# Two-layer trunk kernel: eight pairs of 512-column blocks with a quarter of the contraction by Strassen's scheme

## The chip, the cores and the metric

One Trainium2 chip, one of its cores. The metric is the device time of one execution in microseconds (us); lower is better. The kernel before took 873.62 us in the median of three runs (873.49 to 875.35). Engines: TensorE (PE, its weight loads PEld), VectorE (DVE), ScalarE (ACT), GpSimd (POOL) and SyncE (SP). PE sums its products in PSUM, which has 8 banks of 128 x 512 fp32 numbers.

## The reference

Two layers of a trunk on 256 tokens of width 2048, all in fp32. Layer 0 mixes tokens by differential attention, layer 1 by chunked gated linear attention (GLA). Each layer is `x <- x + W_out(mixer(RMSNorm(x)) * silu(gate))`; cut to the products that matter here:

```python
q, k, v, g = split(h @ w_in, 4)              # layer 0: 2048 x 8192
y = o * silu(g); x = x + y @ w_out           # 2048 x 2048
q, k, v, g, lr = split(h @ w_in, ...)        # layer 1: 1024, 1024, 2048, 2048, 16
o_t = q_t @ state_t                          # state_t = decay * state + k^T v, chunks of 64
x = x + (rmsnorm(o) * silu(g)) @ w_out       # 2048 x 2048
```

## The kernel before, in words

Tokens lie in two halves of 128 (t = 0, 1). A contraction of 2048 is 16 tiles of 128. Every fp32 operand of a product is split into a high part and a remainder, both fp32r: activations once (`aT`, then `bT` in the same memory, and `y`, the input of an out projection, which layer 1 calls `z`), weights as they stream in. `weights()` (L93 to 102) loads a chunk of 128 x 2 x 512 fp32 (two contraction tiles of a block of 512 columns, 512 KB) by a DMA from SP into `raw`, copies it to `hi` on ACT (L100) and writes `lo = raw - hi` on DVE (L101). `raw`, `hi` and `lo` have four buffers each. `stream` (L128 to 132) lists the chunks in the order of use: the four column groups of layer 0's q, k and v, four blocks of its gate, four of its out projection, then k and q, values, gate and out projection of layer 1.

`project()` (L158 to 196) makes one block: two banks of a pool of four (`pj`), one for each half of the tokens, and for each contraction tile and half three matmuls of 128 x 512: high activations by `hi` (L178), remainders by `hi` (L179), high activations by `lo` (L180). That is 96 matmuls a block. k and q of layer 1 are made transposed (L182, L184). While a block runs, `pump()` issues steps of a background list of generators (attention, transposes of x, decay gates, GLA).

After a block its two banks are evacuated: in `gate()` (L431 to 451) by a tanh on ACT (L436) and two products on DVE (L437, L439), then four transposes on PE (L442) and a split of the result (L445 to 451); in an out projection of layer 0 by an addition of x on DVE (L528), after which `transpose_x` (L506 to 522) puts the new x into `bT`; in values by a scaled copy on ACT and a remainder on DVE (L725, L726), after which `gla_values` (L675 to 690) multiplies the attention weights `ATh`, `ATl` with the values into `ps_o` (L681). The last out projection adds x and stores. The last block finishes its bank of t = 0 ahead of the other (`tail`).

The stages follow each other as written, but the order on each engine is set by a scheduler, which goes by priorities (the place in the program) and a timeline of its own; each engine then runs its queue in order. The next block takes the two other banks of the pool:

```python
banks = [bank(pj, "pj"), bank(pj, "pj")]     # L161, pool pj has 4
...
hi, lo = next_weights()                      # L168, one chunk is split ahead
```

Of the kernel before, what the change touches and what calls it, by code (L numbers as in the profile page):

```python
# [16 lines left out]
P = 128  # L17
S = 256
# [11 lines left out]
WARM = 10  # L30


@with_exitstack
def trunk_kernel(
# [29 lines left out]
    pj = ctx.enter_context(tc.tile_pool(name="pj", bufs=4, space=bass.MemoryType.PSUM))  # L64
# [3 lines left out]
    def bank(pool, name):  # L68
        return pool.tile([P, 512], F32, tag=pool.name, name=name)

# [56 lines left out]

    stream = [lambda c=c: first_weights(c) for c in range(NCK)]  # L128
    for w in (aw, awo, bwkq, bwvg, bwo):
        for i in range(w.shape[0]):  # L130
            ck = CK * NB // w.shape[3]
            stream += [w[i, :, k:k + ck, :] for k in range(0, KT, ck)]
# [25 lines left out]
    def project(lhs, token_major, steps=0, before=None, tail=False):  # L158


        banks = [bank(pj, "pj"), bank(pj, "pj")]  # L161
# [3 lines left out]
        for c in range(n):  # L165
# [3 lines left out]
            for kk in range(ck):  # L169
                k = c * ck + kk  # L170
                first, last = k == 0, k == KT - 1
                for t in range(2):
                    sl = slice(t * P, (t + 1) * P)
                    if tail and c == n - 1:
                        continue
# [10 lines left out]
            if tail and c == n - 1:  # L186
                for t in range(2):
                    for kk in range(ck):
                        xh, xl = (lhs[c * ck + kk][:, i, t * P:(t + 1) * P] for i in range(2))
                        nc.tensor.matmul(banks[t], lhsT=xh, rhs=hi[:, kk, :], start=False, stop=False)  # L190
                        nc.tensor.matmul(banks[t], lhsT=xl, rhs=hi[:, kk, :], start=False, stop=False)
                        nc.tensor.matmul(banks[t], lhsT=xh, rhs=lo[:, kk, :], start=False, stop=kk == ck - 1)
# [3 lines left out]
        return banks  # L196

# [10 lines left out]
    def square_sum(blk, pool):  # L208
        for t in range(2):
            jk = pool.tile([P, NB], F32, tag="sq", name="sq", bufs=2 if pool is ta else 1)  # L210
            nc.scalar.activation(jk, xk[:, t, blk * NB:(blk + 1) * NB], AF.Square, accum_out=ssq[:, t, blk:blk + 1])
# [29 lines left out]
    for i in range(2):  # L241
        kl = ta.tile([P, 2, 4, S], F32R, name=f"kl{i}", bufs=1)
# [188 lines left out]
    def gate(banks, o, rh, dst, blk, gains):  # L431

        for t in range(2):
# [10 lines left out]
            yh, yl = (dst[blk // 2][:, blk % 2 * 4:blk % 2 * 4 + 4, i, t * P:(t + 1) * P] for i in range(2))  # L444
            if gains is not None:  # L445
                nc.scalar.activation(yh, ptv, AF.Copy, scale=gains)
                nc.vector.scalar_tensor_tensor(out=yl, in0=ptv, scalar=gains, in1=yh.bitcast(F32),
                                               op0=ALU.mult, op1=ALU.subtract)
            else:
                nc.scalar.activation(yh, ptv, AF.Copy)  # L450
                nc.vector.tensor_tensor(out=yl, in0=ptv, in1=yh.bitcast(F32), op=ALU.subtract)
# [39 lines left out]
    y = None  # L491
    for hg in range(4):
        b = project(aT, True, steps=8)
        if y is None:
            y, yT = operand(["y0", "y1"])
        if hg == 1:
            drain()
        gate(b, o_a[hg], r1h, y, hg, gsub)
    lay_a.close()


    tb_stack = ExitStack()
    tb_ = tb_stack.enter_context(tc.tile_pool(name="tb_", bufs=2))
    _, bT = operand(["aT"])

    def transpose_x(blk):  # L506
        square_sum(blk, tb_)
        yield
        for half in range(2):
            pt = bank(ptr, "pt_x")  # L510
            for j in range(2):
                k = blk * 4 + half * 2 + j
                for t in range(2):
                    nc.tensor.transpose(pt[:, (j * 2 + t) * P:(j * 2 + t + 1) * P], xk[:, t, k * P:(k + 1) * P], ident)
            for j in range(2):
# [8 lines left out]
    for blk in range(4):  # L524
        b = project(yT, True, steps=4)
        cols = slice(blk * NB, (blk + 1) * NB)
        for t in range(2):
            nc.vector.tensor_tensor(out=xk[:, t, cols], in0=b[t], in1=xk[:, t, cols], op=ALU.add)  # L528
        background.append(transpose_x(blk))
# [172 lines left out]


# [9 lines left out]
    for h in range(BH):  # L713
        b = project(bT, False, steps=3)
# [4 lines left out]
    for h in range(BH):  # L719
        b = project(bT, True, steps=4)  # L720
        drain()
        vh = tb_.tile([P, 2, NB], F32R, tag="t4", name="vh", bufs=5)
        vl = tb_.tile([P, 2, NB], F32R, tag="t4", name="vl", bufs=5)
        for t in range(2):
            nc.scalar.activation(vh[:, t, :], b[t], AF.Copy, scale=r2[:, t:t + 1])  # L725
            nc.vector.scalar_tensor_tensor(out=vl[:, t, :], in0=b[t], scalar=r2[:, t:t + 1],  # L726
                                           in1=vh[:, t, :].bitcast(F32), op0=ALU.mult, op1=ALU.subtract)
        v = (vh, vl)
        o = big.tile([P, 2, NB], F32, tag="o", name="ob", bufs=4)
        o_b[h] = o  # L730
        background.append(gla_values(h, v, o))
# [77 lines left out]
```

## Time and profile before

| what | before |
|---|---|
| median of 3 runs | 873.62 us (873.49 to 875.35) |
| the profiled execution | 872.59 us |
| its span in the profile | 870.5 us |
| PE busy | 865.2 us, 99%, 4156 matmuls and transposes |
| DVE busy | 546.1 us, 63%, 824 instructions |
| ACT busy | 468.3 us, 54%, 745 instructions |
| POOL busy | 108.2 us, 12% |
| DMA | 164.40 MB, mean 189 GB/s |

The span runs from the first to the last instruction that the profile shows; the profiled execution's own time holds 2.1 us more. A share is busy time over the span. Matmuls are pipelined, and the duration of one counts its tail: the rows of a busy PE overlap, and the pitch of matmuls is read from their starts. All times in the trace count from the start of the span. A row of the timeline gives start, duration, engine, line, operation and operands (partitions x elements); in brackets behind it stands how long the engine had been idle before, and whose work ended that.

### The profile page before, as it was taken

To read this page: it belongs to the slowest core of one execution; us is meant where nothing else is said; L and a number is where in the kernel's file an instruction comes from. 1 tells how busy PE (TensorE), PEld (TensorE's weight loads), DVE (VectorE), ACT (ScalarE), POOL (GpSimd) and SP (SyncE) were. 2 spreads that over 40 slices of the span, in tenths; PEclk is the share of its full clock that TensorE was granted. 3 is DMA by queue.
4 is the path that set the end of the run, shared out by engine and by line. 5 is a ranking of instruction groups with operands and counts; after the bars stand their busy time and mean duration, and the time that the engine had idled before them with its cause. 6 is when DMAs were issued, how large, how long until landed. Compare 5 with 4: busy or idle time off the path is not lost.

```text
span 870.5 us, 11443 instructions
## 1 busy us (share of the span) xinstructions
PE 865.2 (99%) x4156; PEld 721.8 (83%) x4156; DVE 546.1 (63%) x824; ACT 468.3 (54%) x745; POOL 108.2 (12%) x142
## 2 busy tenths in 40 slices
PE   9999999999999999999999999999999999999998
PEld 6788888888888888888888888888888888888886
DVE  7766775687677676666655658945555565665552
ACT  7756566566656765554545549533444444444331
POOL 3330221023123000103000012300000000000000
PEclk9999999999999999999999999999999999999999
DMA  8886666566665555666666544655565656666771
GB/s 344 292 283 203 182 187 196 180 178 196 186 177 171 182 152 158 197 182 203 200 190 179 182 144 156 200 163 177 172 177 170 183 177 178 189 182 202 211 224 50
DMA packets 47206, 164.40 MB, mean 189 GB/s; under 512 B 5904, under 2 KB 6432, under 8 KB 47152
## 3 DMA queue, kind: packets, MB, share of 16 engines
q1 hardware_dynamic: 43568, 155.47, 58.5%
q0 software_dynamic: 2288, 6.38, 2.5%
q10 hardware_dynamic: 1296, 1.85, 0.6%
q8 instruction: 32, 0.52, 0.2%
q14 instruction: 22, 0.18, 0.1%
HBM read 161.55 MB, written 5.27 MB: 192 GB/s over the span
## 4 chain that ended last, share of the span: by engine, by line
PE 98%; DMA 1%; ACT 0%; DVE 0%; SPq 0%; DVEq 0%; issue 0%
PE pj L178 27%; PE pj L180 27%; PE pj L179 26%; PE pj L182 7%; PE pj L184 3%; PE ps_o L681 1%; PE ps_at L667 1%; PE ps_s L366 1%; PE pt_qk L333 1%; PE pt_y L442 1%; PE ps_s L364 1%; DMA xw<-in_xw 1%; PE pt_a L395 1%; PE po L404 0%; PE ps_lr L578 0%; PE po L406 0%
## 5 line engine op out<-in xcount | busy, mean ns | idle before, releaser
L101 DVE TENSOR_TENSOR lo<-raw,hi 128x1024 fp32r<-128x1024 f32 x280 | 344.0, 1230 | 220.3 <-ACT hi L100 219.7
L100 ACT ACTIVATE hi<-raw 128x1024 fp32r<-128x1024 f32 x280 | 296.2, 1059 | 294.7 <-PE pj L179 246.7
L178 PE MATMUL pj<-hi,aT 128*128 128x512 f32 x768 | 302.8, 396 | 0.0
L180 PE MATMUL pj<-lo,aT 128*128 128x512 f32 x768 | 299.6, 392 | 0.1
L179 PE MATMUL pj<-hi,aT 128*128 128x512 f32 x768 | 299.5, 391 | 0.0
L180 PEld LDWEIGHTS pj<-lo,aT 128*128 128x128 f32 x768 | 144.2, 188 | 30.2 <-DVE lo L124 0.5
L178 PEld LDWEIGHTS pj<-hi,aT 128*128 128x128 f32 x768 | 144.7, 188 | 29.3 <-ACT hi L100 0.6
L179 PEld LDWEIGHTS pj<-hi,aT 128*128 128x128 f32 x768 | 144.7, 188 | 28.7
L178 PE MATMUL pj<-hi,y 128*128 128x512 f32 x252 | 98.9, 392 | 0.0
L180 PE MATMUL pj<-lo,y 128*128 128x512 f32 x252 | 98.3, 390 | 0.0
L179 PE MATMUL pj<-hi,y 128*128 128x512 f32 x252 | 98.1, 389 | 0.0
L182 PE MATMUL pj<-aT,hi 128*128 128x512 f32 x256 | 90.7, 398 | 0.0
L184 PE MATMUL pj<-aT,lo 128*128 128x256 f32 x256 | 71.8, 281 | 0.0
L182 PEld LDWEIGHTS pj<-aT,hi 128*128 128x128 f32 x256 | 48.0, 188 | 11.3
L180 PEld LDWEIGHTS pj<-lo,y 128*128 128x128 f32 x252 | 47.3, 188 | 9.9
L179 PEld LDWEIGHTS pj<-hi,y 128*128 128x128 f32 x252 | 47.3, 188 | 9.6
L178 PEld LDWEIGHTS pj<-hi,y 128*128 128x128 f32 x252 | 47.3, 188 | 9.5
L184 PEld LDWEIGHTS pj<-aT,lo 128*128 128x128 f32 x256 | 48.3, 189 | 0.3
L221 POOL TENSOR_TENSOR rq<-ms,mhalf 128x8 f32<-128x8 f32 x16 | 38.3, 2398 | 34.8 <-DVE ms L323 34.8
L701 POOL TENSOR_TENSOR kq<-kq,rb 128x256 f32<-128x256 f32 x16 | 18.1, 1140 | 75.5 <-DVE kq L699 75.5
L221 POOL TENSOR_TENSOR f<-zz,mhalf 128x2 f32<-128x2 f32 x16 | 11.3, 706 | 91.4 <-DVE zz L413 91.3
L355 POOL DMA_DIRECT2D tb<-skew_d x16 | 9.3, 582 | 96.6 <-DVE nm L371 44.4
(178 smaller groups left out, 681.2 us busy)
## 6 DMA issues: line engine op xcount, KB each, us to landing
raw<-in_aw SPq DMA_DIRECT2D x120, 512.0 KB, 3.7
raw<-in_bwvg SPq DMA_DIRECT2D x64, 512.0 KB, 3.6
raw<-in_awo SPq DMA_DIRECT2D x32, 512.0 KB, 3.6
raw<-in_bwkq SPq DMA_DIRECT2D x32, 512.0 KB, 4.1
raw<-in_bwo SPq DMA_DIRECT2D x32, 512.0 KB, 3.7
xw<-in_xw SPq DMA_DIRECT2D x10, 384.0 KB, 11.4
skew_d<-bias_d POOLq DMA_DIRECT2D x8, 384.0 KB, 6.5
xw<-in_xw SPq DMA_DIRECT2D x3, 768.0 KB, 7.9
```

What stands on the lines that cost most here:

```text
L100: nc.scalar.activation(hi, raw, AF.Copy)
L101: nc.vector.tensor_tensor(out=lo, in0=raw, in1=hi.bitcast(F32), op=ALU.subtract)
L178: nc.tensor.matmul(banks[t], lhsT=xh, rhs=hi[:, kk, :], start=first, stop=False)
L179: nc.tensor.matmul(banks[t], lhsT=xl, rhs=hi[:, kk, :], start=False, stop=False)
L180: nc.tensor.matmul(banks[t], lhsT=xh, rhs=lo[:, kk, :], start=False, stop=last)
L182: nc.tensor.matmul(banks[t], lhsT=hi[:, kk, sl], rhs=lhs[k].rearrange("p a s -> p (a s)"), start=first, stop=False, skip_group_check=True)
L184: nc.tensor.matmul(banks[t][:, 0:S], lhsT=lo[:, kk, sl], rhs=lhs[k][:, 0, :], start=False, stop=last, skip_group_check=True)
L221: nc.gpsimd.tensor_tensor(out=dst, in0=src, in1=mhalf[:, 0:n], op=ALU.pow)
L333: nc.tensor.transpose(pt[:, h * P:(h + 1) * P], qn[:, h * P:(h + 1) * P], ident)
L355: nc.gpsimd.dma_start(tb, bass.AP(tensor=skew_d.tensor, offset=skew_d.offset + (hg * 4 + h) * 384 + 127, ap=[[AH * 384 - 1, P], [1, S]]))
L364: nc.tensor.matmul(pss[t][:, c0:c0 + n], lhsT=q, rhs=qk[:, 8 + t * 4 + h, 0:n], start=True, stop=False)
L701: nc.gpsimd.tensor_tensor(out=dst, in0=dst, in1=rb, op=ALU.mult)
```

## The change

Blocks of the two out projections, of values and of the gate of layer 1 are made as pairs of two adjacent blocks L and L + 1, eight pairs in all. In each pair four of the 16 contraction tiles form a 2 x 2 scheme: token halves by pairs of tiles (A11, A12, A21, A22), and the pairs of tiles by blocks (B11, B12, B21, B22). Strassen's scheme in Winograd's form needs 7 products there instead of 8; a product is 128 x 256 by 256 x 512, six matmuls. The other 12 tiles are made as before (`plain`). Sums on the weight side (u2, u3, and sums in the place of b12 and b22, L246 to 253) are made on DVE from fp32 chunks, and 7 chunks are split where 4 were. Sums on the activation side are made once per mixer (`sums`, in `gate` for the out projections, in `quarter_sums` for values and gate). Four banks with names p0 to p3 take the place of the pool:

- `c` and `e` are the two banks of a group g, `b` and `d` the banks of the other group. `p1` makes the first product in `c` and copies its negative to `b` on ACT (L288). `p7` makes another in `e` and copies it to `s7` in SBUF on ACT (L294).
- `run` adds a product to `c`, makes `d = s7 - c` on DVE (L300), adds to `b`, then alternates plain tiles of the left block (`b`, `d`) with products in `c`; it makes `e = c - s7` on DVE (L307). The left block is evacuated, then the 12 plain tiles of the right block go to `c` and `e`. In the middle of them `p1` and `p7` of the next pair are issued. Group g alternates, so `b` of the next pair is the bank that is `c` of this one.
- The four copies between banks stand under a scheduler priority that is AHEAD = 80 places earlier.
- The memory of layer 0's pool `ta` is held until its out projection has ended, so that loads of layer 1's small weights (`lr_raw` and others, L547 ff. before) come later. Contraction tiles of `awo`, `bwvg` and `bwo` are reordered on the host, and the program's `dynamic_dma_scratch_size` is set to 4096.

The core of the diff (line numbers as L288 count in the changed kernel):

```diff
+AHEAD = 80
-    pj = ctx.enter_context(tc.tile_pool(name="pj", bufs=4, space=bass.MemoryType.PSUM))
+    pj = ctx.enter_context(tc.tile_pool(name="pj", bufs=1, space=bass.MemoryType.PSUM))
...
+    def pj_bank(g, i):
+        return pj.tile([P, 512], F32, tag=f"p{2 * g + i}", name="pj")
...
+    class Pair:
+        def __init__(self, w, L, lhs, S, N, neg, comb, special, left, right):
...
+            n0, n1 = [[self.chunk(i, 2 + c) for c in range(6)] for i in range(2)]
+            self.head = [self.job1, lambda: split(self.u3)]
+            self.mid = [lambda: split(self.u2), self.job2, n0[0], lambda: split(self.b12), n0[1],
+                        lambda: split(self.b22), n0[2], lambda: split(self.u2), *n0[3:]]
+            self.rest = n1
...
+        def load(self):
+            self.b12, self.b22, self.u3, self.u2 = self.special()
+            nc.sync.dma_start(self.b12, self.chunk(1, 0))
+            nc.sync.dma_start(self.b22, self.chunk(1, 1))
...
+        def job1(self):
+            raw, r = self.raw(0)
+            nc.vector.tensor_tensor(out=self.u3, in0=self.b12, in1=self.b22, op=ALU.add)
+            nc.vector.tensor_tensor(out=self.u2, in0=self.u3, in1=raw, op=ALU.add)
+            nc.vector.tensor_tensor(out=self.b12, in0=self.b12, in1=raw, op=ALU.add)
+            return r
...
+        def p1(self):
+            g = self.g = group[0]
+            group[0] = 1 - g
+            self.c, self.e = pj_bank(g, 0), pj_bank(g, 1)
+            self.part(self.c, self.neg, start=True)
+            self.b = pj_bank(1 - g, 0)
+            with tc.high_priority(offset=AHEAD):
+                nc.scalar.activation(self.b, self.c, AF.Copy, scale=-1.0)
+
+        def p7(self):
+            self.part(self.e, lambda j: self.comb(2, j), start=True)
+            self.s7 = gp.tile([P, NB], F32, tag="s7", name="s7", bufs=1)
+            with tc.high_priority(offset=AHEAD):
+                nc.scalar.activation(self.s7, self.e, AF.Copy)
+
+        def run(self, after=None, steps=(1, 1, 1, 1, 1, 1), tail=False):
+            self.part(self.c, lambda j: self.comb(1, j))
+            self.d = pj_bank(1 - self.g, 1)
+            with tc.high_priority(offset=AHEAD):
+                nc.vector.scalar_tensor_tensor(out=self.d, in0=self.c, scalar=-1.0, in1=self.s7,
+                                               op0=ALU.mult, op1=ALU.add)
+            self.part(self.b, self.quarter(1, 0), stop=False)
+            left, right = (self.b, self.d), (self.c, self.e)
+            self.plain(left, 0, True, steps[0])
+            self.part(self.c, lambda j: self.comb(0, j))
+            with tc.high_priority(offset=AHEAD):
+                nc.vector.tensor_tensor(out=self.e, in0=self.c, in1=self.s7, op=ALU.subtract)
+            self.plain(left, 1, False, steps[1])
+            self.part(self.c, lambda j: self.comb(3, j), stop=False)
+            self.plain(left, 2, False, steps[2])
+            self.part(self.d, self.quarter(1, 1), stop=False)
+            for i in range(3, 6):
+                if i == 4 and after is not None:
+                    after.load()
+                self.plain(left, i, False, steps[i])
+            self.left(left)
+            for i in range(6):
+                if after is not None and i == 4:
+                    after.p1()
+                elif after is not None and i == 5:
+                    after.p7()
+                self.plain(right, i, tail and i == 5, steps[i])
+            self.right(right)
...
+    for p, q in zip(pairs_b, pairs_b[1:] + [None]):
+        p.run(q, steps=(1, 1, 1, 1, 0, 0), tail=q is None)
...
+    nc = _bacc.Bacc("TRN2", target_bir_lowering=False, num_devices=1, dynamic_dma_scratch_size=4096)
```

**The order on PE between two projects of values.** A row is a line, an instruction, its output and inputs with shape, and what it waits for; `pj` are banks, a number behind a name tells buffers apart. Before, from the last rows of one block (pj_5632 is its second bank) to the next:

```order
L178 MATMUL pj_5632<-hi_5769,aT_3825 128x512
L179 MATMUL pj_5632<-hi_5769,aT_3825 128x512
L180 MATMUL pj_5632<-lo_5770,aT_3825 128x512
L178 MATMUL pj_5811<-hi_5787,aT_3825 128x512 [waits Activation_49]
L179 MATMUL pj_5811<-hi_5787,aT_3825 128x512
L180 MATMUL pj_5811<-lo_5788,aT_3825 128x512 [waits DVE_49]
L178 MATMUL pj_5812<-hi_5787,aT_3825 128x512
```

Now, from the last rows of the first pair (pj_5485 is `e`) to the second pair (pj_5865 is its `c`; `cb` holds the activations' sums; `ps_o`, `vh`, `vl` belong to the GLA step of the block before):

```order
L276 MATMUL pj_5485<-hi_5898,aT_3877 128x512
L277 MATMUL pj_5485<-hi_5898,aT_3877 128x512
L278 MATMUL pj_5485<-lo_5899,aT_3877 128x512
L895 MATMUL ps_o_5977<-vh_5927,ATh_4593 128x512 [waits Activation_49]
L895 MATMUL ps_o_6018<-vh_5927,ATh_4593 128x512
L895 MATMUL ps_o_5977<-vl_5928,ATh_4593 128x512 [waits DVE_49]
L895 MATMUL ps_o_5977<-vh_5927,ATl_4594 128x512
L895 MATMUL ps_o_6018<-vl_5928,ATh_4593 128x512
L895 MATMUL ps_o_6018<-vh_5927,ATl_4594 128x512
L895 MATMUL ps_o_6018<-vh_5927,ATh_4593 128x512 [waits Activation_49]
L263 MATMUL pj_5865<-hi_5911,cb_2939 128x512 [waits Activation_49]
L265 MATMUL pj_5865<-hi_5911,cb_2939 128x512
```

The next block's first row waited for its split; now the row that adds to `c` waits for ACT, whose copy reads `c`, and seven rows of the GLA step stand between.

**The order on ACT and DVE between two gates of layer 1** (the third block, where the second pair of gates begins). `th` is the tanh and then the gated output, `r2h` the token scale, `ob` the GLA output, pj_6536 and pj_6537 the banks of the block that ends. Before, ACT:

```order
L436 ACTIVATE th_6682<-pj_6536,r2h_4641 128x512 [waits PE_49]
L100 ACTIVATE hi_6743<-raw_6742 128x1024 [waits DMAHW5_49,DVE_49,PE_49]
L436 ACTIVATE th_6693<-pj_6537,r2h_4641 128x512 [waits PE_49]
L100 ACTIVATE hi_6761<-raw_6760 128x1024 [waits DMAHW6_49,DVE_49,PE_49]
L100 ACTIVATE hi_6779<-raw_6778 128x1024 [waits DMAHW7_49,DVE_49,PE_49]
```

and DVE:

```order
L101 TENSOR_TENSOR lo_6726<-raw_6724,hi_6725 128x1024 [waits DMAHW4_49,PE_49,Activation_49]
L437 SCALAR_TENSOR_TENSOR th_6682<-th_6682,ob_5990 128x512 [waits Activation_49]
L439 SCALAR_TENSOR_TENSOR th_6682<-pj_6536,r2h_4641,th_6682 128x512 [waits DVE_49]
L101 TENSOR_TENSOR lo_6744<-raw_6742,hi_6743 128x1024 [waits DMAHW5_49,PE_49,Activation_49]
L437 SCALAR_TENSOR_TENSOR th_6693<-th_6693,ob_5990 128x512 [waits Activation_49]
```

Now (pj_6238 and pj_6239 are `c` and `e` of the first pair, pj_6620 and pj_6621 those of the second; pj_6634, the second pair's `b`, is the bank of pj_6238; `comb` and `cf` are sums of the gated output, `special` holds weight sums), ACT:

```order
L294 ACTIVATE s7_6664<-pj_6621 128x512 [waits PE_49]
L592 ACTIVATE th_6682<-pj_6238,r2h_4719 128x512 [waits PE_49]
L142 ACTIVATE hi_6731<-special_5434 128x1024 [waits DVE_49,PE_49]
L592 ACTIVATE th_6693<-pj_6239,r2h_4719 128x512 [waits PE_49]
L582 ACTIVATE comb_6503<-cf_6538 128x4x128 [waits DVE_49]
L288 ACTIVATE pj_6634<-pj_6620 128x512 [waits DVE_49]
```

and DVE:

```order
L335 TENSOR_TENSOR cf_6538<-pt_y_6509,cf_6538 128x128 [waits DVE_49]
L593 SCALAR_TENSOR_TENSOR th_6682<-th_6682,ob_5933 128x512 [waits Activation_49]
L246 TENSOR_TENSOR special_6836<-special_6834,special_6835 128x1024
L143 TENSOR_TENSOR lo_6732<-special_5434,hi_6731 128x1024 [waits PE_49,Activation_49]
L595 SCALAR_TENSOR_TENSOR th_6682<-pj_6238,r2h_4719,th_6682 128x512 [waits DVE_49]
```

On ACT the copy of `c` to `b` (L288) now stands behind both tanh of the block that ends and a split; on DVE a weight sum and a split stand between the two products that read pj_6238.

## Rows read from the trace of the kernel before

**Rows 1.** The page, parts 1 and 2: busy time, and the clock in 40 slices.
```profile
PE 865.2 (99%) x4156; PEld 721.8 (83%) x4156; DVE 546.1 (63%) x824; ACT 468.3 (54%) x745; POOL 108.2 (12%) x142
...
PE   9999999999999999999999999999999999999998
...
PEclk9999999999999999999999999999999999999999
```

**Rows 2.** The page, part 4: the chain that ended last, by engine.
```profile
PE 98%; DMA 1%; ACT 0%; DVE 0%; SPq 0%; DVEq 0%; issue 0%
```

**Rows 3.** Busy time by window, first output projections, then values to end.
```profile
core 0: us, PE busy (x) PEld busy (x) DVE busy (x) ACT busy (x) POOL busy (x), PEclk, DMA share, GB/s
408.00:500.00 92.00, 92.00 (x435) 76.64 (x434) 54.27 (x65) 47.20 (x67) 5.67 (x12) 1.00 0.63 189
600.00:866.00 266.00, 266.00 (x1204) 220.85 (x1203) 142.64 (x147) 113.96 (x131) 4.34 (x8) 1.00 0.60 176
```

**Rows 4.** Timeline of PE in an output projection: start, duration, engine, line.
```profile
446.63 0.39 PE L179 MATMUL pj<-hi,y 128*128 128x512 f32 x1
...
449.35 0.39 PE L179 MATMUL pj<-hi,y 128*128 128x512 f32 x1
```

**Rows 5.** Who waited for whom: us in total, times, longest.
```profile
ACT hi L100 <- PE pj L179: 246.7, 163, 2.1
```

**Rows 6.** Groups of instructions on ACT: busy us, mean ns, idle before.
```profile
L100 ACT ACTIVATE hi<-raw 128x1024 fp32r<-128x1024 f32 x280 | 296.2, 1059 | 294.7 <-PE pj L179 246.7 <-PE pj L182 17.1 <-issue 12.5
...
L698 ACT ACTIVATE kq<-pj 128x256 f32<-128x256 f32 x16 | 6.0, 376 | 12.0 <-PE pj L184 12.0
...
L725 ACT ACTIVATE vh<-pj,r 128x512 fp32r<-128x512 f32 x8 | 5.5, 686 | 4.9 <-PE pj L180 4.9
...
L450 ACT ACTIVATE y<-pt_y 128x512 fp32r<-128x512 f32 x8 | 4.7, 590 | 1.2 <-PE pt_y L442 1.2
```

**Rows 7.** Groups of instructions on DVE, same columns.
```profile
L101 DVE TENSOR_TENSOR lo<-raw,hi 128x1024 fp32r<-128x1024 f32 x280 | 344.0, 1230 | 220.3 <-ACT hi L100 219.7 <-PE pj L179 0.3
...
L439 DVE SCALAR_TENSOR_TENSOR th<-pj,r2h,th 128x512 f32<-128x512 f32 x8 | 6.0, 752 | 0.3
...
L528 DVE TENSOR_TENSOR xk<-pj,xk 128x512 f32<-128x512 f32 x8 | 5.4, 688 | 0.0
```

**Rows 8.** The page, part 6: DMA issues, KB each, us to landing.
```profile
raw<-in_bwvg SPq DMA_DIRECT2D x64, 512.0 KB, 3.6
```

**Rows 9.** Timeline behind a project's last matmul: a gate, of PE, ACT and DVE.
```profile
754.67 0.39 PE L180 MATMUL pj<-lo,aT 128*128 128x512 f32 x1
...
755.10 0.69 ACT L436 ACTIVATE th<-pj,r2h 128x512 f32<-128x512 f32 x1 [1.21 <-PE pj L180]
755.68 1.05 ACT L100 ACTIVATE hi<-raw 128x1024 fp32r<-128x1024 f32 x1
756.63 0.68 ACT L436 ACTIVATE th<-pj,r2h 128x512 f32<-128x512 f32 x1
...
755.82 0.69 DVE L437 SCALAR_TENSOR_TENSOR th<-th,ob 128x512 f32<-128x512 f32 x1 [0.67 <-ACT th L436]
756.54 0.75 DVE L439 SCALAR_TENSOR_TENSOR th<-pj,r2h,th 128x512 f32<-128x512 f32 x1
```

**Rows 10.** Timeline of PE around four transposes, and around three state products.
```profile
786.72 0.60 PE L442 MATMUL pt_y<-ident,th 128*128 128x128 f32 x4
...
787.39 0.39 PE L178 MATMUL pj<-hi,y 128*128 128x512 f32 x1
...
620.36 0.39 PE L681 MATMUL ps_o<-vh,ATh 128*128 128x512 f32 x1
...
621.04 0.39 PE L178 MATMUL pj<-hi,aT 128*128 128x512 f32 x1
```

**Rows 11.** Timeline of PE at the start: the warm-up matmuls.
```profile
1.23 4.45 PE L81 MATMUL ps_idle<-zero 128*128 128x512 bf16 x10 [1.23 <-DVE zero L78]
```

More of the change, by code (lines that the diff above doesn't have):

```diff
@@ L156, in drain, with project @@
             pump()
-    def project(lhs, token_major, steps=0, before=None, tail=False):
-        banks = [bank(pj, "pj"), bank(pj, "pj")]
+    def project(lhs, token_major, steps=0, before=None):
+        banks = [pj_bank(group[0], i) for i in range(2)]
+        group[0] = 1 - group[0]
         n = NCK if token_major else NCK // 2
@@ L185, in project @@
                                          start=False, stop=last, skip_group_check=True)
[L186 to L192, printed above, removed]
             want = (c + 1) * steps // n
@@ L490, in trunk_kernel @@
         background.append(attention(hg, qk, kl, v, o))
[L491 to L504, printed above, removed]
     def transpose_x(blk):
-        square_sum(blk, tb_)
+        square_sum(blk, gp)
         yield
@@ L521, in transpose_x @@
                                                in1=bT[k][:, 0, :].bitcast(F32), op0=ALU.mult, op1=ALU.subtract)
-            yield
[L524 to L529, printed above, removed]
+                if blk == 0:
+                    nc.scalar.activation(af[:, 2 * j:2 * j + 2, :].rearrange("p a s -> p (a s)"), p, AF.Copy, scale=g)
@@ new lines, in trunk_kernel, with add_x, f, neg_in_place @@
+    cb = big.tile([P, 2, 5, 2, P], F32R, tag="cb", name="cb")
+    def add_x(blk):
+        def f(banks):
+            cols = slice(blk * NB, (blk + 1) * NB)
+            for t in range(2):
+                nc.vector.tensor_tensor(out=xk[:, t, cols], in0=banks[t], in1=xk[:, t, cols], op=ALU.add)
+            background.append(transpose_x(blk))
+        return f
+    ya, yT = [], []
+    def neg_in_place(views, S_):
+        return lambda j: tuple(views[S_[j][0]][:, a, 0:P] for a in range(2))
+    comb_a = ta.tile([P, 2, 4, 2, P], F32R, tag="kl0", name="comb_a", bufs=1)
@@ L704, in trunk_kernel @@
+    for i in range(2 * BH):
+        stream += block(bwkq, i)
+    last = [stream.pop() for _ in range(NCK // 2)][::-1]
+    stream += last[:2] + pairs_b[0].head[:1] + last[2:3] + pairs_b[0].head[1:] + last[3:]
+    stream += pairs_stream(pairs_b)
     for h in range(BH):
@@ L713, in trunk_kernel @@
     for h in range(BH):
-        b = project(bT, False, steps=3)
+        b = project(bT, False, steps=3, before=early(pairs_b[0], (2, 3)) if h == BH - 1 else None)
         evac(b, h, qTb, 1.0 / 16)
@@ L777 @@
     wb = a["b_w_in"][0]
+    first = [0, 2, 1, 3, *range(4, KT)]
     arrays = {
```

239 lines of the change are left out of this document (191 added, 48 removed).

## The prediction

> **What bounds the kernel now.** I read the page's first two parts, then the chain of waits, then the windows of the four stages that change, then the groups of instructions. TensorE is busy for 865 of 870.5 us and its granted clock reads full speed in every slice [rows 1]; the chain that ended last runs 98% through PE [rows 2]. In both stretches that the change rewrites PE is busy for the whole window, 92.00 of 92 us and 266.00 of 266 us, while DVE is busy for 59% and 54% of them and ACT for 51% and 43% [rows 3]. So the time is the number of matmuls times their pitch. The pitch is read between starts, not from the 0.39 us of one row, which counts the pipeline's tail: 12 matmuls from 446.63 to 449.35, 0.2267 us each [rows 4]. PE has no slack: every wait that is put on it is paid in full. ACT and DVE have some: ACT waited 163 times, 246.7 us in all, for PE to give back a hi buffer [rows 5], so the splits run as far ahead as four buffers let them.
>
> **What goes.** In each of eight pairs 8 products of 6 matmuls become 7. 48 matmuls fewer, 3072 to 3024 of the wide ones in the order: 48 x 0.2267 = 10.9 us off PE, all of it on the path. Transposes, value products and the low rank stage stay.
>
> **What comes beside PE.** Per pair three more splits (7 instead of 4): 3 x 1.06 = 3.2 us on ACT [rows 6] and 3 x 1.23 = 3.7 on DVE [rows 7]; four additions of 128x1024, which I price as L101's 1.23, 4.9 on DVE; two bank copies on each of the two engines, 1.2 on ACT (as L450, 0.59) and 1.4 on DVE (as L528 and L439). That is 10.0 us on DVE in a pair of some 44 us, 23% on top of 54 to 59%: below the bound on average, so I take nothing for it except lateness at seams, below. Cover gone, it would cost what DVE is over. Two more sums of quarter tiles per mixer (eight on DVE of a quarter of L528's width, between 0.17 and 0.69 each) hide the same way. The same bytes are loaded; the pair's two extra tiles are issued on SP two chunks before the left blocks end and are wanted some 16 us later, against 3.6 us to land [rows 8], so SP's queue holds nothing up. lr_raw now waits on POOL until the first pairs' tiles are free; by the order ACT comes to it about as it lands, and three chunks of weights are split ahead. Smaller DMA scratch: POOL is busy for 12%; 0, at most 1 us.
>
> **What comes on the path: the seam.** The pair's first product is made in bank c while the previous right blocks are still being summed. Its negative goes into bank b, and b is the bank of the previous right block's first half. So the copy waits for that bank's evacuation, and the next PE rows wait for the copy, since they add to c and b. The order shows the chain at every seam: last matmul on the bank, evacuation (ACT, DVE, or both), mostly one hi split of 1.06 us ahead of the copy on ACT, often the evacuation of the second bank too, then the copy, then PE. Before, the next project had the other two banks and went straight on: the gate at 755 took from 755.10 to 757.29 with PE running throughout [rows 9].
>
> Lags: PE's last slot on the bank ends at 754.90, tanh starts at 755.10, 0.20 later; ACT to DVE 0.03; a queued instruction starts 0.1 before the one ahead ends [rows 9]. No copy from bank to bank is in the trace; between L698's 0.38 for half the width and L725's 0.69 with a pointer [rows 6], I take L450's 0.59, the same width without a pointer. The bounds move the eight seams by -1.7 and +0.8 us.
>
> Zero is the end of the last matmul on the bank. PE still has three matmuls of the other bank, 0.68.
> - **Output A, first pair:** tanh to 0.89, split to 1.85, s7's copy to 2.34, a split to 3.3, second tanh to 3.9, copy to 4.4. PE has five matmuls and four transposes (0.44, 786.72 to 787.39 less a matmul [rows 10]): 2.9 idle.
> - **Output A, second pair:** ACT's split waits for its buffer until 0.61, runs to 1.7, the copy to 2.2, PE goes on at 2.25; idle 2.25 - 0.68 - 0.2 (two transposes) = 1.4. DVE, with the quarter sums in its queue, reaches the addition of x about 1 us late by my count: 2.4.
> - **Values, first pair:** evacuation of q, split, second evacuation, copy: 2.4, with 0.6 of work: 1.8.
> - **Values, second pair, and gates, first:** vh to 0.89, split to 1.85, vh to 2.43, copy to 2.93. But seven products of the state (0.68 for three, 620.36 to 621.04 [rows 10]) stand in PE's order ahead of the wait: 0.7 idle each.
> - **Gates, second pair:** on DVE the first product with tanh (0.69), an addition (1.23), a split (1.23) and only then the second product (0.75) stand one behind the other: 0.92 to 4.6; copy to 5.2, PE at 5.25, idle 4.1. The sums of the first gate put 6.4 us of work on DVE after the last buffer that it waits for; I count it 1 us late: 5.1.
> - **Output B, first pair:** tanh to 0.89, the two products to 2.3, ACT's second tanh to 2.43, copy to 2.93: 1.9. **Second pair:** as output A's without lateness: 1.6.
>
> Sum 2.9 + 2.4 + 1.8 + 0.7 + 0.7 + 5.1 + 1.9 + 1.6 = 17.1 us idle. The later copies (d and e) have six to twelve matmuls, 1.4 to 2.7 us, between them and their reader, and I follow them in time for it: 0, at most 0.3 each, 5 us for sixteen.
>
> [...]
>
> **The sum.** The profiled execution took 872.6 us. 872.6 - 10.9 + 17.1 = 878.8. The median of three runs, 873.62, is 1.0 above it, so in the median 879.8, slower by 0.7%.
>
> **Rivals.**
> 1. **Short seams, faster.** If the splits that stand ahead of the copy in ACT's and DVE's queues are done before zero, a seam is evacuation, copy and lags alone: 1.4, 0.7, 1.1, 0.1, 0.1, 1.9, 1.9 and 0.9 in the order of the list, about 8 us, and 873.6 - 10.9 + 8.0 = 870.7. It decides when idle time at the seams falls under 10.9 us, 1.36 each. For it speaks that the copies carry a priority; against it that the order puts a split between evacuation and copy in seven of eight, and that its buffer is freed after zero. Chance 0.15.
> 2. **In between.** Seams of some 11 us, the lateness gone and the waits a third shorter: 873.6, within 0.2% (what a measurement of this kernel can tell from no change). Chance 0.11.
> 3. **DVE late everywhere.** If DVE does not keep up with 77 to 82% and every pair loses another 1.2 us at its tight first third, where nine splits and two bank copies meet 15 us of matmuls: 879.8 + 9.6 = 889. DVE's own 12.5 us of work there speak against it. Chance 0.06.
> 4. **The clock swings.** If after each stop PE ran at half rate for as long as it stood, half of 17.1 us would be lost again: 888. [...] The continuous work between stops, 44 us, speaks against it. Chance 0.06.
>
> The forecast keeps 0.62. Faster by over 0.2% (below 871.9): 0.15. Within 0.2%: 0.11. Slower (above 875.4): 0.62 + 0.12 = 0.74. The range: the copies' price and the d and e copies give 878 to 885 around the forecast; the lower end goes to 870.5, which takes in the middle case and half of the first rival, the upper to 886.5, short of the last two. What is left out is some 0.08 and 0.10.
>
> **What would show it.** In the changed profile PE should have eight idle stretches, each ended by ACT's line 288, in two out projections, values and second gates, some 17 us in all, the longest (about 5 us) in the middle of the gates; 48 fewer matmuls at the same pitch; DVE at 70 to 73% of the span. If these stretches sum to less than 10.9 us, the forecast is wrong, and the place to look is whether ACT's splits came before the evacuation. If PE also waits in mid pair for L300, L307 or a lo split, it is the third rival; if the pitch after a stop is 0.45 us, the fourth.

## The result, and the profile after

The changed kernel took **880.32 us** in the median of four runs (879.93 to 883.22), before 873.61; the ratio is 1.0079 (95% interval 1.0054 to 1.0104): slower by 0.8%. The profiled execution is the longest of the four, 883.22 us with a span of 881.1. The page's first lines, then the same two windows as in [rows 3]:

```profile
PE 862.8 (98%) x4108; PEld 714.2 (81%) x4108; DVE 626.4 (71%) x931; ACT 506.8 (58%) x801; POOL 107.0 (12%) x142
...
PE   9999999999999999998999999999999998999997
```

```profile
408.00:500.00 92.00, 91.03 (x417) 74.59 (x417) 67.93 (x87) 53.93 (x80) 10.05 (x22) 0.99 0.63 194
600.00:866.00 266.00, 258.71 (x1149) 211.40 (x1148) 194.72 (x207) 140.07 (x164) 4.52 (x9) 0.99 0.58 178
```

PE has 48 instructions fewer (4108 for 4156 of [rows 1]), DVE 107 more and 71% of the span. The slices of PE, all nines before but the last, now have an 8 in two places. In the windows PE is busy for 91.03 of 92 us and 258.71 of 266, and the clock reads 0.99: 8 us of stops where [rows 3] had none, and something at the lower clock. DVE rose from 54.27 to 67.93 us in the first window and from 142.64 to 194.72 in the second, and has 71 us left there.

Whom PE waited for (engine, tile and line, and who released it; us in total, times, longest; before the only entry was the start, 1.2 us):

```profile
PE pt_y L598 <- DVE th L595: 6.8, 3, 3.9
PE pj L263 <- ACT pj L288: 3.0, 3, 1.4
...
PE ps_at L881 <- POOL kq L915: 1.2, 1, 1.2
PE pt_x L663 <- DVE xk L695: 0.6, 1, 0.6
```

The copy (L288) ends three of these waits, one in each pair of output A and one in output B's second; a gate's product on DVE (L595) ends three, in output A's first pair, the gates' second and output B's first, since PE's order there puts the first half's transposes (L598) ahead of the rows on `c`. How long PE stood at a seam (the place where one block ends and a pair begins) is read from the starts of neighbouring matmuls, less the matmul's own 0.227 and the transposes between:

| seam | forecast, us | stop in the trace, us |
|---|---|---|
| output A, first pair | 2.9 | 2.8 |
| output A, second | 2.4 | 1.35 |
| values, first | 1.8 | 1.7 |
| values, second; gates, first | 0.7 each | 0.5 each |
| gates, second | 5.1 | 4.0 |
| output B, first | 1.9 | 1.9 |
| output B, second | 1.6 | 1.6 |
| sum | 17.1 | 14.3 |

The last matmul starts 9.8 us later than before (875.89 for 866.07). That is 10.9 us of products gone, 14.3 of stops, 3.1 for two stretches at the lower clock (below), and 3.3 us in many gaps of under 0.5 us, which no run took apart. Another 0.8 lies behind the last matmul.

The simplest seam is the last one, second pair of output B; PE's, ACT's and DVE's timelines:

```profile
833.98 0.39 PE L278 MATMUL pj<-lo,z 128*128 128x512 f32 x1
...
834.65 0.39 PE L278 MATMUL pj<-lo,z 128*128 128x512 f32 x1
836.45 0.50 PE L263 MATMUL pj<-hi,comb 128*128 128x512 f32 x1 [1.41 <-ACT pj L288]
...
834.85 1.06 ACT L142 ACTIVATE hi<-special 128x1024 fp32r<-128x1024 f32 x1 [1.19 <-PE pj L277]
...
835.82 0.58 ACT L288 ACTIVATE pj<-pj 128x512 f32<-128x512 f32 x1
...
834.40 1.37 DVE L970 TENSOR_TENSOR ot<-pj,xk 128x512 f32<-128x512 f32 x2
```

Bank `c`'s last product starts at 833.98; DVE adds x (L970, both halves, until 835.77). ACT meanwhile splits a chunk until 835.91, after waiting for its buffer, and only then copies `c` to `b` (L288); the copy ends at 836.40, and PE, which has stood since its last row, goes on at 836.45. The longest seam is the one in the middle of the gates:

```profile
738.70 0.39 PE L278 MATMUL pj<-lo,aT 128*128 128x512 f32 x1
...
743.64 0.63 PE L598 MATMUL pt_y<-ident,th 128*128 128x128 f32 x4 [3.87 <-DVE th L595]
744.16 0.75 PE L263 MATMUL pj<-hi,cb 128*128 128x512 f32 x1
...
739.13 0.69 ACT L592 ACTIVATE th<-pj,r2h 128x512 f32<-128x512 f32 x1 [0.67 <-PE pj L278]
739.71 1.04 ACT L142 ACTIVATE hi<-special 128x1024 fp32r<-128x1024 f32 x1
...
743.53 0.58 ACT L288 ACTIVATE pj<-pj 128x512 f32<-128x512 f32 x1 [1.68 <-DVE th L595]
...
739.88 0.68 DVE L593 SCALAR_TENSOR_TENSOR th<-th,ob 128x512 f32<-128x512 f32 x1
740.48 1.22 DVE L246 TENSOR_TENSOR special<-special 128x1024 f32<-128x1024 f32 x1
741.62 1.22 DVE L143 TENSOR_TENSOR lo<-special,hi 128x1024 fp32r<-128x1024 f32 x1
742.75 0.74 DVE L595 SCALAR_TENSOR_TENSOR th<-pj,r2h,th 128x512 f32<-128x512 f32 x1
```

Zero, the end of the last matmul on the bank, is 738.93. DVE's two products on `th` (739.88 and 742.75) have a weight sum (L246) and a split (L143) between them; the copy starts when the second ends, 743.53. PE's row on `c` follows at 744.16, 5.23 us behind zero.

The two short seams have another wait. In values' second pair (the gates' first is alike) PE's, then ACT's rows are:

```profile
646.61 0.73 PE L895 MATMUL ps_o<-vh,ATh 128*128 128x512 f32 x2
...
648.67 0.46 PE L263 MATMUL pj<-hi,cb 128*128 128x512 f32 x1
...
645.87 0.69 ACT L925 ACTIVATE vh<-pj,r 128x512 fp32r<-128x512 f32 x1 [0.72 <-PE pj L278]
...
647.97 0.59 ACT L288 ACTIVATE pj<-pj 128x512 f32<-128x512 f32 x1
```

PE's last row on the block starts at 646.12. It then stands for the first GLA row (L895), which reads `vh`; that evacuation ends at 646.56, and the row starts at 646.61. The rest of the 0.5 us is a wait for `vl`. The copy ends at 648.56, and the row on `c` starts at 648.67, right behind the seven GLA rows. So here the copy holds nothing up.

What follows in the trace of PE shows the clock. Behind output A's first stop a few matmuls run at the old pitch, 0.23 us, then the pitch is 0.427 (six from 406.44 to 409.00), then 0.23 again; the windows of this stretch and of the one behind the gates give the granted clock, 0.50 and 0.51 (PE busy, clock, DMA share, GB/s):

```profile
405.69 0.39 PE L265 MATMUL pj<-hi,comb_a 128*128 128x512 f32 x1
...
406.44 0.63 PE L265 MATMUL pj<-hi,comb_a 128*128 128x512 f32 x1
...
409.00 0.63 PE L265 MATMUL pj<-hi,y 128*128 128x512 f32 x1
...
410.04 0.39 PE L277 MATMUL pj<-hi,y 128*128 128x512 f32 x1
```

```profile
406.30:409.70 3.40, 3.40 (x10) 0.50 0.32 118
744.20:747.60 3.40, 3.40 (x9) 0.51 0.00 0
```

### The profile page after: what moved, and what is told of

It is laid out like the page before. It is cut to its first block, busy times and chain, and to the rows that moved or that the text cites. A ratio compares the mean times of both kernels' runs of the same rounds, so it can differ in the third digit from the quotient of the medians.

```text
span 881.1 us, 11539 instructions
## 1 busy us (share of the span) xinstructions
PE 862.8 (98%) x4108; PEld 714.2 (81%) x4108; DVE 626.4 (71%) x931; ACT 506.8 (58%) x801; POOL 107.0 (12%) x142
## 4 chain that ended last, share of the span: by engine, by line
PE 51%; DVE 2%; ACT 1%; issue 0%; POOL 0%; DVEq 0%; ACTq 0%
PE pj L276 10%; PE pj L277 10%; PE pj L278 10%; PE pj L198 7%; PE pj L200 3%; PE pj L263 3%; PE pj L265 3%; PE pj L266 3%; PE ps_o L895 1%; PE ps_at L881 1%; PE pt_y L598 0%; PE ps_lr L792 0%; DVE lo L108 0%; PE pt_x L663 0%; DVE lo L143 0%
## 5 line engine op out<-in xcount | busy, mean ns | idle before, releaser
L108 DVE TENSOR_TENSOR lo<-raw,hi 128x1024 fp32r<-128x1024 f32 x248 | 303.9, 1230 | 123.5 <-ACT hi L107 122.1
L107 ACT ACTIVATE hi<-raw 128x1024 fp32r<-128x1024 f32 x248 | 261.6, 1058 | 222.5 <-PE pj L277 84.5
L194 PE MATMUL pj<-hi,aT 128*128 128x512 f32 x512 | 202.8, 398 | 0.0
L195 PE MATMUL pj<-hi,aT 128*128 128x512 f32 x512 | 200.0, 392 | 0.0
L196 PE MATMUL pj<-lo,aT 128*128 128x512 f32 x512 | 199.7, 394 | 0.0
L194 PEld LDWEIGHTS pj<-hi,aT 128*128 128x128 f32 x512 | 96.5, 189 | 20.0 <-issue 0.6
L196 PEld LDWEIGHTS pj<-lo,aT 128*128 128x128 f32 x512 | 96.2, 188 | 20.3 <-DVE lo L131 0.5
L195 PEld LDWEIGHTS pj<-hi,aT 128*128 128x128 f32 x512 | 96.5, 188 | 19.1 <-DVE aT L129 0.2
L276 PE MATMUL pj<-hi,aT 128*128 128x512 f32 x192 | 75.1, 391 | 0.0
L277 PE MATMUL pj<-hi,aT 128*128 128x512 f32 x192 | 75.0, 391 | 0.0
L278 PE MATMUL pj<-lo,aT 128*128 128x512 f32 x192 | 72.5, 391 | 0.0
L143 DVE TENSOR_TENSOR lo<-special,hi 128x1024 fp32r<-128x1024 f32 x40 | 49.0, 1225 | 10.3 <-ACT hi L142 8.7
L142 ACT ACTIVATE hi<-special 128x1024 fp32r<-128x1024 f32 x40 | 42.4, 1059 | 21.3 <-PE pj L277 9.4
L276 PEld LDWEIGHTS pj<-hi,aT 128*128 128x128 f32 x192 | 36.1, 188 | 7.5
L277 PEld LDWEIGHTS pj<-hi,aT 128*128 128x128 f32 x192 | 36.1, 188 | 7.4
L278 PEld LDWEIGHTS pj<-lo,aT 128*128 128x128 f32 x192 | 36.0, 188 | 7.4
L276 PE MATMUL pj<-hi,y 128*128 128x512 f32 x96 | 37.9, 395 | 0.0
```

Of the source, the lines that this page charges most:

```text
L107: nc.scalar.activation(hi, raw, AF.Copy)
L108: nc.vector.tensor_tensor(out=lo, in0=raw, in1=hi.bitcast(F32), op=ALU.subtract)
L142: nc.scalar.activation(hi, raw, AF.Copy)
L143: nc.vector.tensor_tensor(out=lo, in0=raw, in1=hi.bitcast(F32), op=ALU.subtract)
```

## The experiments

Three theories. **A**, the prediction's: PE stands at a seam because `b` is a bank of the block before, and its copy stands behind that bank's evacuation in queues that run in order. **B**: DVE's 15% more work is what comes late, and the seam only shows it. **C**: the clock behind the stops costs as much as the stops. The ratios are to the kernel before on the same chip, 872.95 to 873.29 us in the median.

**The priority.** With AHEAD at 0 or at 1000 the order of instructions is row for row that of 80 on all five engines: the priority moves nothing. It was not timed.

**e1: bank b set apart** in five pairs (output A, second gates, output B).

```diff
...
-            self.b = pj_bank(1 - g, 0)
+            self.b = bank(psc, "pb") if self.own else pj_bank(1 - g, 0)
...
```

> Bank b of five pairs (both pairs of output A, second pair of gates, both of output B) is a bank that no earlier block uses, so the copy of c to b waits for no evacuation. Theory A (PE stands at the seam because b is the bank of the block before and its copy stands behind an evacuation in queues that run in order): the five stops that the trace shows there, 2.8 + 1.35 + 4.3 + 1.9 + 1.6 = 12.0 us, go; about 1 us comes back where d waits for the other bank; the half-rate stretches behind the longest stops (1.5 us each) go with them: 880.3 - 12.0 + 1.0 - 1.5 = 867.8, faster than before the change. Theory B (DVE, 15% more loaded, is what is late; the seam only shows it): the waits move to d's copy (L300) and to lo splits some rows later, and no more than 4 us are won: 876 or more. Theory C (most of the loss is the clock behind stops, not the stops): the time falls by much more than the stops' 12 us.

Measured 873.04 us, ratio 1.0002 (0.9992 to 1.0011). Part of output A comes out wrong in this run and in e18 (last section); no instruction of the program depends on the values, and e12, where nothing is wrong, takes the argument to its end. The five stops of 11.6 us are gone as such, and the clock is 1.00, but less was won than A expected (7.3 us from 880.3): PE's waits have new names.

```profile
PE pj L276 <- DVE pj L300: 3.1, 3, 1.4
...
PE pb L278 <- DVE lo L108: 1.1, 1, 1.1
```

PE now waits for L300, the copy to `d`: `d` is the second bank of the block before, evacuated later still. The stops around these rows are 1.65, 2.9 and 1.3 us, 5.85 in all, where I had expected 1. The middle one, in the gates, is not all a wait for `d`: 1.1 us of it is a wait for a `lo` split ahead of a row on `b`, and 0.6 one for a gate's product. So the waits moved to L300 and a `lo` split, as B said, and more was won than the 4 us that B allows. This run alone doesn't decide between a second bank and a late DVE. A's forecast of 867.8 missed by 5.2 us, because freeing one bank hands the wait to the next.

**e18: the same, with a matmul of zeros ahead of b.**

```diff
...
+            self.b = bank(psc, "pb") if self.own else None; self.own and self.L == 0 and nc.tensor.matmul(self.b, lhsT=zero[:, 0:P], rhs=zero, start=True, stop=True)
+            self.part(self.c, self.neg, start=True); self.b = self.b or pj_bank(1 - g, 0)
...
```

> Bank b alone set apart in five pairs, as in the first experiment, but a matmul of zeros first writes all 512 columns of that bank (twice in the program, 0.23 us each). Theory A: the same stops as there, before rows on d, 5.85 us in all: 873.0 + 0.45 = 873.5.

873.98 us, ratio 1.0013 (1.0003 to 1.0023): as expected, with the same stops before rows on `d`.

**e12: b and d set apart.**

```diff
...
+            self.b, self.d = (bank(psc, "pb"), bank(psc, "pd")) if self.own else (None, None)
+            self.part(self.c, self.neg, start=True); [nc.tensor.matmul(x, lhsT=zero[:, 0:P], rhs=zero, start=True, stop=True) for x in (self.b, self.d) if self.own == 2]
...
-            self.d = pj_bank(1 - self.g, 1)
+            self.d = self.d or pj_bank(1 - self.g, 1)
...
```

> In the five pairs b and d both lie in banks that no earlier block of the chain uses (two matmuls of zeros write them whole before the first pair, 0.45 us). In the run with b alone set apart, stops of 1.65, 2.9 and 1.3 us stood before rows on d, whose copy (L300) waited for the second bank's evacuation. Theory A: these 5.85 us go too: 873.0 - 5.85 + 0.45 = 867.6, 0.6% faster than before the change, with PE's only stop of over 1 us at the first pair of values (1.5, waiting for POOL). Theory B (DVE, with 15% more work, holds PE): the stops only move on, to lo splits: 872 to 873.

867.26 us, ratio 0.9936 (0.9922 to 0.9949): faster than both kernels. PE's list of waits, the one at the start of the program and the only other of 1 us or more, and the first part of its page:

```profile
PE ps_idle L88 <- DVE zero L85: 1.2, 1, 1.2
PE ps_at L882 <- POOL kq L916: 1.2, 1, 1.2
```

```profile
PE 857.3 (99%) x4110; PEld 711.5 (82%) x4110; DVE 624.6 (72%) x931; ACT 507.0 (59%) x801; POOL 108.2 (13%) x142
```

DVE carries as much as in the changed kernel (72%), and PE runs through all five seams, the waits for `lo` splits gone too: B falls. By the starts of the last matmul e12 is 5.6 us ahead of the kernel before (860.49 for 866.07). That is 10.9 us of products, less 2.7 of stops at the three seams that kept their banks, 0.45 of zeros and 2.2 in small gaps that no run took apart. So the products were worth most of their 10.9 us, and the shared banks took that back.

**e6: the copy on DVE instead of ACT.**

```diff
-                nc.scalar.activation(self.b, self.c, AF.Copy, scale=-1.0)
+                nc.vector.tensor_scalar(out=self.b, in0=self.c, scalar1=-1.0, scalar2=None, op0=ALU.mult)
```

> The copy of c to b is made on DVE instead of ACT. Theory A says that the place in the in-order queue decides: by the order the copy now stands behind a split of 1.23 us more in output A's second pair (+1.8 us), behind two more instructions in the middle of the gates (+1.2) and behind a split and a first product in output B's first pair (+1.8), and nearer to its evacuation in values and first gates (-0.3 each) and output A's first (-0.15): 880.3 + 4.0 = 884.3, with the stops at those places longer by these amounts. If the copy's engine and the queue didn't matter, only the evacuation: 880.3. Theory B (DVE's load): slower by 8 x 0.7 us spread over the pairs, 886, without a pattern by seam.

888.71 us, ratio 1.0179 (1.0162 to 1.0196). The stops changed seam by seam, as the queue's order said: output A's first 2.7 (-0.1), its second 2.5 (+1.1, expected +1.8), gates 5.1 (+1.1, expected +1.2), output B's first 3.8 (+1.9, expected +1.8), its second 1.6 (0). DVE and PE at output B's first seam:

```profile
790.67 0.75 DVE L595 SCALAR_TENSOR_TENSOR th<-pj,r2h,th 128x512 f32<-128x512 f32 x1
791.34 1.22 DVE L143 TENSOR_TENSOR lo<-special,hi 128x1024 fp32r<-128x1024 f32 x1
792.47 0.69 DVE L593 SCALAR_TENSOR_TENSOR th<-th,ob 128x512 f32<-128x512 f32 x1
793.07 0.69 DVE L288 TENSOR_SCALAR pj<-pj 128x512 f32<-128x512 f32 x1
...
793.91 0.77 PE L263 MATMUL pj<-hi,comb 128*128 128x512 f32 x1 [1.71 <-DVE pj L288]
```

The copy (793.07) stands behind a split and the second half's first product, and PE's row behind the copy. The total is 4 us more than the stops give, which the clock explains at least in part: in this kernel's trace the clock fell twice for 6.8 us, not for 3.4 (same columns as above).

```profile
741.20:748.00 6.80, 4.96 (x13) 0.50 0.11 43
792.40:799.20 6.80, 5.29 (x13) 0.50 0.45 175
```

**e10: output A in plain blocks.** Its two pairs go back to `project`; six pairs stay.

```diff
...
-    out_a[0].run(out_a[1])
-    out_a[1].run()
+    for blk in range(4):
+        add_x(blk)(project(yT, True, steps=4))
...
```

> Output A goes back to four plain blocks, the six other pairs stay. Theory A: 12 matmuls of 0.2267 come back, +2.7 us, and two seams of 2.8 and 1.35 go, and the half-rate stretch behind the first of them in the runs that had one: 880.3 - 1.4 = 878.9, or 877.4 with that. If seams were hidden elsewhere and the products counted alone: 880.3 + 2.7 = 883.0.

878.92 us, ratio 1.0065 (1.0050 to 1.0080). The two stops are gone and the others unchanged (4.0, 1.9, 1.6): by the rows a pair costs its seam and gives back 1.36 us, and in output A the seams (4.15 us) cost more than two pairs give (2.7). The time excludes the 883.0 of the rival, but doesn't show this difference: 1.4 us is no more than one stretch at the lower clock takes (1.6 by the rows of the changed kernel), and two of the four executions have a mean clock of 0.994 (879.61 and 879.68 us), for 0.998 in the others (878.23 and 877.81).

**e4, e16, e13 and e17: the clock.** e4 and e16 are one kernel; 13 matmuls of zeros run in the stop of the gates, started by an instruction on POOL behind the tanh.

```diff
...
+            nc.gpsimd.tensor_scalar(out=zw[:, 0:1], in0=src[:, 0:1], scalar1=0.0, scalar2=None, op0=ALU.mult)
+            zz = bank(psc, "ps_warm")
+            for _ in range(n):
+                nc.tensor.matmul(zz, lhsT=zw, rhs=zero, start=True, stop=True)
...
```

> 13 matmuls of zeros (2.9 us) fill the stop in the middle of the gates, started by a one-column instruction on POOL behind the first tanh; the stop itself stays. Theory C (the granted clock falls behind a stop, and the stretch at the lower level costs as much again as the rows show, 8 matmuls at 0.43 instead of 0.23 us): the clock column reads 1.00 through this seam and 1.5 us are won, less some 0.4 us by which the first product on DVE now waits for POOL: 879.2. Theory A alone, with the clock playing no part: 880.7.

> The changed kernel once more, unchanged, as the measure for the others of this chip: 880.3, with one or two stretches of 3.4 us at the lower clock, behind the stops of output A's first pair and of the gates.

> The kernel with 13 matmuls of zeros in the stop of the gates once more, on the same chip as the changed kernel. Theory C (a stop is followed by a stretch at the lower clock, which costs on top of it): the clock stays at 1.00 through this seam and the time is 1 to 1.6 us under that of the changed kernel. Without C: 0.4 us over it.

> The changed kernel as it is, as the measure for these two: 880 to 882, with one to three stretches at the lower clock.

e4 took 880.56 us (ratio 1.0084, 1.0069 to 1.0099); the changed kernel again, e13, 882.04 on another chip (1.0106, 1.0093 to 1.0120); on one chip e16 took 880.04 (1.0085, 1.0066 to 1.0103) and the changed kernel, e17, 880.33 (1.0083, 1.0068 to 1.0098). The window around the gates' seam, of e16 and then of e17 (PE busy, clock, DMA share, GB/s):

```profile
738.00:746.00 8.00, 6.57 (x31) 1.00 0.42 128
```

```profile
738.00:746.00 8.00, 4.58 (x15) 0.79 0.32 110
```

With PE kept at work the clock stays at 1.00 there (in e4 the pitch behind this seam is 0.23 us, as before it), and without it falls, 0.79 on average over the 8 us. In the rows one such stretch costs eight matmuls of 0.2 us, 1.6 us. In the medians it doesn't show: e16 and e17 agree within their intervals. The clock's mean over an execution was 0.996 to 0.994 in e13 and 0.998 in e17. 3.4 us at 0.50 lower the mean of 881 us by 0.002, so by my estimate the same kernel met two or three such stretches on one chip and one on the other; the medians, 882.04 and 880.33, are 0.2% apart. C is right in that such a stretch follows the longest stop, and small beside A: 3.1 us where the stops are 14.3.

**e15: what holds the first seam of values?** There the trace names POOL's product of q.

```diff
-            nc.gpsimd.tensor_tensor(out=dst, in0=dst, in1=rb, op=ALU.mult)
+            (nc.vector if h == BH - 1 and store is qTb else nc.gpsimd).tensor_tensor(out=dst, in0=dst, in1=rb, op=ALU.mult)
```

> On top of the change the last block of q is multiplied by its row scale on DVE instead of POOL. In the changed kernel PE stood 1.47 us before the first pair of values, and the trace names POOL's product as what released it; the copy of c to b (L288) ended 0.4 us later, as PE's first row on c began. Theory A (the copy is what holds this seam too, as forecast with 1.8 us): the stop keeps its length within 0.4 us, and its releaser becomes ACT's L288 or DVE; the time is that of the changed kernel on this chip. Rival (POOL is what holds it, and the copy is covered): 1.2 us less.

881.12 us, ratio 1.0094 (1.0077 to 1.0111), against 880.33 for e17 on the same chip. PE and ACT at this seam, in the changed kernel and then in e15:

```profile
598.00 0.43 PE L881 MATMUL ps_at<-kq,kez 128*128 128x64 f32 x2 [1.22 <-POOL kq L915]
598.44 0.50 PE L263 MATMUL pj<-hi,cb 128*128 128x512 f32 x1
...
597.78 0.60 ACT L288 ACTIVATE pj<-pj 128x512 f32<-128x512 f32 x1
```

```profile
596.67 0.41 PE L881 MATMUL ps_at<-kq,kez 128*128 128x64 f32 x2 [0.97 <-DVE kq L915]
597.37 0.50 PE L263 MATMUL pj<-hi,cb 128*128 128x512 f32 x1 [0.29 <-ACT pj L288]
...
596.71 0.60 ACT L288 ACTIVATE pj<-pj 128x512 f32<-128x512 f32 x1
```

In the first, PE's row on `c` (598.44) follows the copy's end (598.38) as closely as it follows the attention products that waited for POOL. In e15 q is ready sooner, and PE waits a second time, for L288. The stop is 1.7 us in both: the copy holds this seam too, under another's name. The time is 0.8 us over e17's; three of e15's four executions have a mean clock of 0.996, two stretches at the lower clock by the same estimate, and e17's have 0.998, one.

**e19: b of the first values pair set apart as well**, on top of e12 and e15's edit.

> On top of the kernel with b and d set apart, b of the first pair of values lies in a bank of its own too, and the last block of q is scaled on DVE. Theory A: the stop of 1.7 us before values falls to what POOL or DVE leave of it, 0.5 us or less: 867.3 - 1.2 = 866.1. Against it: the attention weights' products now have one bank instead of two in this stretch and may wait for their own evacuation; then 867 to 868.

865.26 us, ratio 0.9911 (0.9896 to 0.9926): the fastest, 15 us under the changed kernel. The stop before values is gone whole, where I had left 0.5 us of it, and the products of attention weights did not wait. Of the 0.8 us by which the time is under the forecast that explains 0.5.

**e5: the scratch alone**, on the kernel before.

> The kernel before with dynamic_dma_scratch_size of 4096 and nothing else: no difference, 0 to 1 us by the prediction.

872.79 us, ratio 0.9996 (0.9987 to 1.0005): no effect, as forecast.

## Why the prediction was right, and where it was not

- **What bounds the kernel, and that PE has no slack:** right. Every stop found its way into the time until the banks were set apart; then most of the 10.9 us of 48 matmuls came out as time (5.7 us under the kernel before in e12 and 8.0 in e19, where three and two seams still stop).
- **The prices:** right. The copies on ACT took 0.590 us (forecast 0.59, taken between bounds of 0.38 and 0.69), those to `d` on DVE 0.697 (0.72), the weight sums 1.224 (1.23):

```profile
L288 ACT ACTIVATE pj<-pj 128x512 f32<-128x512 f32 x8 | 4.7, 590 | 1.7 <-DVE th L595 1.7
```

```profile
L246 DVE TENSOR_TENSOR special<-special 128x1024 f32<-128x1024 f32 x8 | 9.8, 1224 | 3.3 <-DMA special<-in_bwvg 2.5 <-DMA special<-in_awo 0.4 <-DMA special<-in_bwo 0.4
...
L300 DVE SCALAR_TENSOR_TENSOR pj<-pj,s 128x512 f32<-128x512 f32 x8 | 5.6, 697 | 3.5 <-PE pj L266 3.3
```

- **The seams:** the mechanism is shown by e12 and e6, and for values' first pair by e15 and e19. Six of eight came within 0.2 us, but values' second pair and the gates' first (0.7, measured 0.5) by another wait than forecast: PE stood for `vh` and `vl`, not for the copy, so there the size is luck. In the gates the forecast had the copy's end at 5.2 and PE at 5.25 us behind zero, and the trace has 5.18 and 5.23. What failed there and in output A's second pair is the term I put on top, "1 us late" on DVE: in the gates DVE began its first product as the tanh ended (739.82 and 739.88), and output A's addition of x began 0.7 us behind zero (450.24) and ended under ACT's split, which holds the copy up anyway:

```profile
450.89 1.06 ACT L142 ACTIVATE hi<-special 128x1024 fp32r<-128x1024 f32 x1 [1.22 <-PE pj L277]
...
450.94 0.69 DVE L695 TENSOR_TENSOR xk<-pj,xk 128x512 f32<-128x512 f32 x1
```

  A lateness on DVE of that size costs nothing there, and to add it to ACT's time in full was a slip of the sum. These two are 2.1 of the 2.8 us by which 17.1 was too much.
- **What the sum left out:** the clock (3.1 us in the profiled execution) and small gaps (3.3 us, of which some 2 are there in e12 too, where PE runs through the five seams that were set apart). I gave both no term, the clock because no row before showed it. The d and e copies, taken at nothing and bounded at 5, cost nothing: no row on PE waits for L300 or L307. Against the profiled execution, 883.22, the sum of 878.8 is 4.4 short; against the median, where three of four executions have a mean clock of 0.998 (one stretch by the estimate above), 0.5. So that 879.8 is so near 880.32 is in part luck: too much lateness stood where the clock and the gaps should have.
- **Releasers:** I expected ACT's L288 at the end of each stop; three show L595, one POOL, and two end with `vh` and `vl`. In the first four the chain is the one forecast, and the name depends on what PE's order has in front; in the last two it isn't.
- **The rivals:** short seams would have needed no split between evacuation and copy, and the trace has one at every seam. DVE late everywhere fell with e12. The clock's swing is real but came behind the long stops: in the profiled execution a fall to 0.50 and 0.51 follows output A's first (2.8 us) and the gates' second (4.0), none the six stops of 1.9 us and less. The fourth rival put some 8 us on it, half of all stops; the rows have 3.1. (Its sign was a pitch of 0.45 us, and in these two stretches the pitch is 0.427. The ten warm-up matmuls of [rows 11] have the same from start to start; their 4.45 us count the tail of the last.)

## What to carry to other kernels

Where one engine is full, a scheme that saves instructions on it is worth what its joints leave: here 10.9 us of products less 14.3 of stops. Before counting the products saved, follow the first bank of each group from its last reader to its first new writer through every in-order queue between, and give banks that are filled by copy a place whose reader was done long ago; then do the same for the next bank, since freeing one hands the wait to the other (873.04 us with one bank set apart, 867.26 with both). A bank that is filled by a copy here also wanted a product over all its columns ahead of the copy: without it 384 of the 512 columns lost the copy in output A's left blocks (e1), with it none (e12, e19; last section). A scheduling priority doesn't shorten a chain of dependences (AHEAD at 0, 80 and 1000 gives one order); the order of instructions tells before a run whether it moves anything.

## What the runs showed of the hardware that was not expected

- The granted clock of the changed kernel read 0.50 and 0.51 for 3.4 us behind the stops of output A's first pair (2.8 us) and of the gates (4.0), when PE was already at work again, and 1.00 behind its stops of 1.9 us and less (440 to 480, 600 to 700, 791 to 800 and 834 to 870 us). The stop of 4.0 us in the gates was followed by such a stretch in every trace that has it (in e17 0.51 from 741.90 to 745.30); the 2.8 us in output A, the same in each, by one in two further traces (e4, whose stop in the gates is filled, with a mean clock of 0.998, and e13 with 0.996) and by none in three (e15 and e17 with 0.998, e16 with 1.000). Where the stops were 5.1 and 3.8 us (e6) it read 0.50 for 6.8 us, from within the stop. By my estimate from the mean clock, 0.002 a stretch, one kernel had one such stretch in an execution on one chip (e17, 0.998) and two or three on another (e13, 0.996 to 0.994).
- In e1, and for one of two banks in e18, part of what ACT had copied into bank `b` is missing from the sum that the following products built there, in the left blocks of output A. In such a bank the last products before the copy were attention scores: a sum begun on 256 of the 512 columns, then one begun on 128 others. Where a product over all 512 columns came ahead of the copy (both banks in e12 and e19) nothing is missing. How much is missing can be told from the relative error of the result (root of the summed squares), 0.2434 in e1 and 0.1722 in e18. If in the reference, computed with the same inputs, the copied values are left out on the 384 columns outside the 128 that were begun last, in both left blocks, its result changes by 0.2434, and in the second block alone by 0.1722; if they are left out only on the 128 columns that neither sum had touched, by 0.143 and 0.101. So 384 columns lost the copy, among them the 256 of the earlier sum; why they did, no run shows.
